# Other start columns for the two halves of the split weights, by group

## The chip, the cores and the metric

The kernel runs on one core of a Trainium2 chip. The metric is device time in microseconds (us), from the start to the end of one execution; lower is better. The time before is the median of three runs, 2103.79 us (2103.69 to 2105.68).

## The reference, cut to what matters

Two layers of a hybrid block, on 256 tokens of width 2048, all in float32. Each layer normalises, projects, mixes in three ways (spatial gating, attention in a window, mLSTM), projects back, and ends in a gated feed-forward part of width 5632:

```python
def hybrid_layer(x, ...):
    hn = rmsnorm(x, norm1_g)
    proj = hn @ w_in                          # 2048 -> 4360
    a_u, a_v, b_q, b_k, b_v, c_qk, c_v, c_o, c_i, c_f = jnp.split(proj, split_idx, axis=-1)
    ...
    mixed = jnp.concatenate([mix_a, mix_b, mix_c], axis=-1)
    h = x + mixed @ w_out                     # 2048 -> 2048
    hn2 = rmsnorm(h, norm2_g)
    return h + (jax.nn.silu(hn2 @ w_gate) * (hn2 @ w_up)) @ w_down   # 2048 -> 2 x 5632 -> 2048
```

Nearly all the arithmetic is in these five products with weights, some 190 MB of weights per layer.

## The kernel before, in words

**Splitting.** TensorE multiplies in a rounded float32 format (fp32r). To keep float32 accuracy each weight and each activation is used as a sum of a high part and a low part. Weights arrive by DMA as `raw` tiles of 128 x 2048 values. `wsplit` (L184 to L193) takes 1024 columns at a time, called a split here: ScalarE (ACT) casts them to the high part `wh` (L191), VectorE (DVE) subtracts that from `raw` to get the low part `wl` (L192).

**The ring.** `wh` and `wl` are two long tiles (L180) of `NSPLIT * SK * CW + LINE` = 4128 columns of 4 bytes. They hold four places for splits, used in turn: split number `i` modulo 4 writes the columns from `i * 1024 + o`, where `o` is an offset that `PLACE` (L41) gives for `wh` and for `wl`, by the form of the product that will read the split:

```python
PLACE = dict(A=(20, 20), B=(12, 12), C=(24, 28))
wh, wl = [t[:, i * SK * CW + o:(i + 1) * SK * CW + o] for t, o in zip(parts, PLACE[form])]
```

An offset of one column is 4 bytes, so (24, 28) starts `wh` 96 bytes and `wl` 112 bytes behind a multiple of 4096 bytes from the tile's start.

**The three forms** (`gemm_steps`, L224 to L307) are three ways to multiply by a split. On TensorE one operand is loaded into the array (the weights of the array, a LDWEIGHTS instruction, PEld in the profile), the other one streams through it (MATMUL).

- Form A (`mm_a`, L239 to L249), tokens on the partitions of the result: the activations are loaded, `wh` and `wl` stream, 512 columns each. Three matmuls (a triple) for each block of 128 inputs and 128 tokens.
- Form B (`mm_f`, L269 to L271), features on the partitions: 128 columns of `wh` or `wl` are loaded, 256 tokens stream. Three matmuls for each block.
- Form C (`mm_f`, L265 and L266): 128 columns of `wh` are loaded and the high and the low activations stream behind one another, 512 columns; then 128 columns of `wl` are loaded and the 256 high activations stream. Two matmuls (a pair) for each block.

**Which group uses which.** A group is one product by 512 columns of weights. In each layer, in this order: `c_q`, `c_k` (form B), a small group of 264 columns (form A), `c_v`, the two halves of `b_q`, `a_v` (form A), `a_u` (form B), `c_o` (form A), four groups of `w_out` (three C, one B), then the feed-forward part in two halves: 12 gate and up groups (form C, each with 256 columns of gate and 256 of up), four groups of `w_down`; 10 gate and up groups, four of `w_down`. The loop over gate and up groups is at L995 to L1024, their product at L999. A group of 16 blocks with form C has 64 pairs and uses 8 splits, so each such group starts at the first place of the ring.

**What sets the order.** TensorE takes the matmuls in the order in which the program is written. The splits are written under a raised priority (L189), so that the scheduler puts the cast and the subtraction among the other work of ACT and DVE ahead of need; the exact position comes out of the scheduler. A cast waits until TensorE has read what stood in its columns.

**Activations.** They lie in `xn_sb` (normalised input), in `big` tiles of 8192 bytes per partition, and, for the last gate and up groups of a half, in `slot` tiles of 4224 bytes per partition.

Of the kernel before, what the change touches and what calls it, by code (L numbers as in the profile page):

```python
# [27 lines left out]
CW = 512  # L28
WK = 4
SK = 2  # L30
# [10 lines left out]
PLACE = dict(A=(20, 20), B=(12, 12), C=(24, 28))  # L41
# [7 lines left out]
OFF = dict(a_u=0, a_v=512, b_q=1024, b_k=2048, b_v=2176, c_q=2304, c_k=2816, c_v=3328, c_o=3840, c_i=4352, c_f=4356)  # L49
G_CQ, G_CK, G_CV, G_Q0, G_Q1, G_AV, G_AU, G_CO = range(8)  # L50
GROUP_COLS = [OFF["c_q"], OFF["c_k"], OFF["c_v"], OFF["b_q"], OFF["b_q"] + 512, OFF["a_v"], OFF["a_u"], OFF["c_o"]]


_p = 0
# [18 lines left out]
def hybrid(ctx: ExitStack, tc: tile.TileContext, xt, win, wsm, wout, wgu, wdn, prm, cst, fgb, yt):  # L73
# [48 lines left out]
    def kchunks(w, order=None):  # L122

        order = range(KT // WK) if order is None else order
        return [(w[c], list(range(c * WK, (c + 1) * WK))) for c in order]
# [54 lines left out]
    parts = [wp.tile([P, NSPLIT * SK * CW + LINE], F32R, tag=k, name=k) for k in ("wh", "wl")]  # L180
    split_no = [0]
    last_split = [None]

    def wsplit(raw, lo, n, form, pieces=1):  # L184
        i = split_no[0] % NSPLIT
        split_no[0] += 1
        wh, wl = [t[:, i * SK * CW + o:(i + 1) * SK * CW + o] for t, o in zip(parts, PLACE[form])]
        m = n // pieces
        with tc.high_priority(HIPRI):  # L189
            for i in range(0, n, m):  # L190
                A.copy(wh[:, i:i + m], raw[:, lo + i:lo + i + m])  # L191
                last_split[0] = V.tensor_tensor(wl[:, i:i + m], raw[:, lo + i:lo + i + m],  # L192
                                                wh[:, i:i + m].bitcast(F32), op=ALU.subtract)  # L193
        return wh, wl
# [9 lines left out]
    def gemm(*args, **kw):  # L204

        steps = gemm_steps(*args, **kw)
        while True:
            try:
                next(steps)
            except StopIteration as end:  # L210
                return end.value
# [9 lines left out]
                    out[i] = end.value  # L221
        return [out[i] for i in range(len(steps))]

    def gemm_steps(form, chunks, xs, cols=CW, ready=None, step0=SK, split=0):  # L224

        ps = [bank(), bank()] if split else gbank()
        if form == "C":
            up = [bank(), bank()]
            tiles = [ps[:, 0:512], ps[:, 512:1024], up[0], up[1]]
        nk = sum(len(k) for _, k in chunks)
        done = 0

        def mm_a(wh, wl, j, kt, first, last, cs=range(NC)):  # L239
            xh, xl = xs(kt)  # L240
            h = wh[:, j * cols:(j + 1) * cols]
            lo = wl[:, j * cols:(j + 1) * cols]
            for c in cs:
                o = ps[c][:, 0:cols] if split else ps[:, c * 512:c * 512 + cols]
                xhc = xh[:, c * P:(c + 1) * P]
                xlc = xl[:, c * P:(c + 1) * P]
                T.matmul(o, xhc, h, start=first, stop=False)  # L247
                T.matmul(o, xhc, lo, start=False, stop=False)  # L248
                T.matmul(o, xlc, h, start=False, stop=last)  # L249

        def mm_first(wh, wl, kt):

            xh, xl = xs(kt)
            for i, (w, x) in enumerate(((wh, xh), (wh, xl), (wl, xh))):
                for f in range(4):
                    T.matmul(ps[:, f * S:(f + 1) * S], w[:, f * P:(f + 1) * P], x, start=i == 0 and f % 2 == 0,
                             stop=False, skip_group_check=True)

        def mm_f(wh, wl, j, kt, f, first, last):
            xh, xl = xs(kt)  # L260
            h = wh[:, j * CW + f * P:j * CW + (f + 1) * P]
            lo = wl[:, j * CW + f * P:j * CW + (f + 1) * P]
            if form == "C":
                o = tiles[f]
                T.matmul(v3(o, 2), h, xs(kt, True), start=first, stop=False, skip_group_check=True)  # L265
                T.matmul(o[:, 0:S], lo, xh, start=False, stop=last, skip_group_check=True)  # L266
            else:
                o = ps[:, f * S:(f + 1) * S]
                T.matmul(o, h, xh, start=first and f % 2 == 0, stop=False, skip_group_check=True)  # L269
                T.matmul(o, h, xl, start=False, stop=False, skip_group_check=True)  # L270
                T.matmul(o, lo, xh, start=False, stop=last, skip_group_check=True)  # L271

        second = []
        for ci, (src, kts) in enumerate(chunks):
            apart = ci >= len(chunks) - split
            raw, step = wload(src, len(kts) * cols), step0 if ci == 0 else SK
            late = form != "A" and ci == len(chunks) - 1
            held = []
            for s0 in range(0, len(kts), step):
                ks = kts[s0:s0 + step]  # L280
                wh, wl = wsplit(raw, s0 * cols, len(ks) * cols, form, 2 if done == 0 and ready is ready_x else 1)
                if ready is not None:
                    ready(ks)
                for j, kt in enumerate(ks):
                    first, last = done == 0, done == nk - 1
                    done += 1
                    if form == "A":
                        mm_a(wh, wl, j, kt, first, last, range(1) if apart else range(NC))
                        if apart:
                            second.append((wh, wl, j, kt, first, last))  # L290
                    elif late:
                        held.append((wh, wl, j, kt, first, last))
                    elif first and ready is ready_x:
                        mm_first(wh, wl, kt)
                    else:
                        for f in range(4):
                            mm_f(wh, wl, j, kt, f, first, last)
                if not late:
                    pump()
                if step0 == 1 and ci == 0 and s0 + step < len(kts):  # L300
                    yield
            if late:
                for f in range(4):
                    for wh, wl, j, kt, first, last in held:
                        mm_f(wh, wl, j, kt, f, first, last)
                    if f % 2 == 1:
                        pump()  # L307
            if ci < len(chunks) - 1:
                yield
        for a in second:  # L310
            mm_a(*a, range(1, NC))
        return (ps, up[0], up[1]) if form == "C" else ps
# [624 lines left out]
    for l in range(DEPTH):  # L937
# [1 line left out]
        st = {}  # L939

        def inproj(i, form):
            return gemm(form, kchunks(win[l, i]), xn)

        if l == 0:
            start(rstd_of(st, True))
            ps, ps1 = in_turn(gemm_steps("B", kchunks(win[l, G_CQ]), xn, ready=ready_x, step0=1),
                              gemm_steps("B", kchunks(win[l, G_CK]), xn, step0=1))
        else:
            start(rstd_of(st))
            ps = inproj(G_CQ, "B")  # L950
# [16 lines left out]
        ps = inproj(G_AU, "B")  # L967
# [23 lines left out]
        for half, (c0, c1) in enumerate(HALVES):  # L991
# [3 lines left out]
            for g in range(ng):  # L995
                if half == 0 and g == 0:
                    st = {}
                    start(rstd_of(st))
                ps, u0, u1 = gemm("C", kchunks(wgu[l, 2 * c0 + g]), xn)  # L999
                need(st, "rbc")  # L1000
                rbc = st["rbc"]
                ts = slot()
                t = ts[:, 0:1024]
                pv = v3(ps, 2)
                A.copy(v3(t[:, 0:512], 2), pv[:, :, S:2 * S])
                V.tensor_tensor(v3(t[:, 0:512], 2), pv[:, :, 0:S], v3(t[:, 0:512], 2), op=ALU.add)
                for j, u in enumerate((u0, u1)):
                    tj = t[:, 512 + j * S:512 + (j + 1) * S]
                    A.copy(tj, u[:, S:2 * S])
                    V.tensor_tensor(tj, u[:, 0:S], tj, op=ALU.add)  # L1010
                V.tensor_tensor(v3(t, 4), v3(t, 4), bc4(rbc), op=ALU.mult)
                A.activation(t[:, 0:512], t[:, 0:512], AF.Silu)
                V.tensor_tensor(t[:, 0:512], t[:, 0:512], t[:, 512:1024], op=ALU.mult)
                if g >= 2 * NBIG:
                    a = slot(F32R)
                    small_act.append(a)
                    av = a[:, 0:1024].rearrange("p (k i t) -> p k i t", k=2, i=2)
                else:
                    if g % 2 == 0:
                        pair = big()  # L1020
                    av = pair[:, 2 * (g % 2):2 * (g % 2) + 2]
                A.copy(av[:, :, 0, :], v3(t[:, 0:512], 2))
                V.tensor_tensor(av[:, :, 1, :], v3(t[:, 0:512], 2), av[:, :, 0, :].bitcast(F32), op=ALU.subtract)
                release(ts)  # L1024
                act.append(av)
# [116 lines left out]
```

## Time and profile before

| what | value |
| --- | --- |
| median of three runs | 2103.79 us (2103.69 to 2105.68) |
| the profiled execution's own time | 2104.66 us |
| its span, first to last instruction | 2102.9 us |
| TensorE busy in the span | 2091.1 us (99%), 12492 matmuls |
| TensorE weight loads busy | 1845.9 us (88%) |
| VectorE / ScalarE busy | 1330.2 us (63%) / 1014.5 us (48%) |
| mean granted TensorE clock | 0.999 of 2.4 GHz |
| DMA | 390.78 MB, mean 186 GB/s |

TensorE's matmuls overlap: one starts while its predecessor still drains, so a matmul that the profile gives 390 ns adds less than that to the time. What a matmul costs is read from the distance between two starts, or from the length of a stretch that holds a known number of them. The table's last rows are shares of a span in which TensorE is nearly always busy; whether the other engines matter is read from what TensorE waits for.

### The profile page before, as it was taken

The numbers are of one execution on the slowest core, as the hardware profiler recorded it, in microseconds if no ns is written. First come the engines' busy times: TensorE is split into PE (matmuls) and PEld (weight loads), VectorE is DVE, ScalarE is ACT, GpSimd is POOL, SyncE is SP. The second block draws the span as 40 slices with busy tenths as digits, with TensorE's granted clock in tenths as the row PEclk, the third lists the DMA queues.
The fourth block names the chain that finished last, engine by engine and source line by source line (L and its number), as shares of the span: only waits on it lengthen the run. The fifth ranks groups of instructions, "written<-read, shape, count | busy, mean of one in ns | idle before, by whom it ended". The sixth has DMA issues, their size and how long they took to land.

```text
span 2102.9 us, 30395 instructions
## 1 busy us (share of the span) xinstructions
PE 2091.1 (99%) x12492; PEld 1845.9 (88%) x12492; DVE 1330.2 (63%) x1827; ACT 1014.5 (48%) x1334; POOL 9.1 (0%) x14
## 2 busy tenths in 40 slices
PE   9999999999999999999999999999999999999998
PEld 9888899888888888888998888988888888888886
DVE  6776666656654566566566766666665555656695
ACT  5655544544443344444445554454444433444443
POOL 0000000000000000000000000000000000000000
PEclk9999999999999999999999999999999999999999
DMA  6544555555555555555546435555555555555653
GB/s 255 211 140 151 177 187 191 187 199 184 198 186 195 182 199 185 196 188 193 184 144 215 141 131 190 191 190 189 191 195 187 199 181 199 186 195 188 212 192 128
DMA packets 56731, 390.78 MB, mean 186 GB/s; under 512 B 6544, under 2 KB 7312, under 8 KB 10512
## 3 DMA queue, kind: packets, MB, share of 16 engines
q1 hardware_dynamic: 56304, 388.33, 52.8%
q8 instruction: 97, 1.59, 0.3%
q10 hardware_dynamic: 288, 0.52, 0.1%
q14 instruction: 42, 0.34, 0.0%
HBM read 386.73 MB, written 2.10 MB: 185 GB/s over the span
## 4 chain that ended last, share of the span: by engine, by line
PE 99%; DVE 0%; issue 0%; DMA 0%; ACT 0%; SPq 0%; POOLq 0%; DVEq 0%; POOL 0%
PE g L265 22%; PE m L265 22%; PE g L266 11%; PE m L266 11%; PE g L247 5%; PE g L248 5%; PE g L249 5%; PE g L269 4%; PE g L271 4%; PE g L270 4%; PE m L566 1%; PE m L620 1%; PE m L609 1%; PE m L247 0%; PE m L248 0%; PE m L249 0%
## 5 line engine op out<-in xcount | busy, mean ns | idle before, releaser
L192 DVE TENSOR_TENSOR wl<-raw,wh 128x1024 fp32r<-128x1024 f32 (+2 forms) x741 | 886.7, 1205 | 600.6 <-ACT wh L191 592.2
L191 ACT CAST wh<-raw 128x1024 fp32r<-128x1024 f32 (+2 forms) x741 | 758.8, 1033 | 865.5 <-PE m L265 528.8
L265 PE MATMUL g<-xn_sb,wh 128*128 128x512 f32 x1408 | 510.8, 390 | 0.0
L265 PE MATMUL m<-xn_sb,wh 128*128 128x512 f32 x1408 | 510.8, 390 | 0.0
L266 PE MATMUL g<-xn_sb,wl 128*128 128x256 f32 x1408 | 391.8, 278 | 0.0
L266 PE MATMUL m<-xn_sb,wl 128*128 128x256 f32 x1408 | 391.8, 278 | 0.0
L265 PEld LDWEIGHTS m<-xn_sb,wh 128*128 128x128 f32 x1408 | 264.3, 188 | 55.5
L265 PEld LDWEIGHTS g<-xn_sb,wh 128*128 128x128 f32 x1408 | 264.2, 188 | 55.4
L266 PEld LDWEIGHTS m<-xn_sb,wl 128*128 128x128 f32 x1408 | 264.3, 188 | 0.1
L266 PEld LDWEIGHTS g<-xn_sb,wl 128*128 128x128 f32 x1408 | 264.3, 188 | 0.1
L265 PE MATMUL g<-big,wh 128*128 128x512 f32 x512 | 187.7, 391 | 0.0
L265 PE MATMUL m<-big,wh 128*128 128x512 f32 x512 | 187.4, 390 | 0.0
L247 PE MATMUL g<-wh,xn_sb 128*128 128x512 f32 (+1 forms) x384 | 147.8, 385 | 0.0
L248 PE MATMUL g<-wl,xn_sb 128*128 128x512 f32 (+1 forms) x384 | 143.8, 375 | 0.0
L249 PE MATMUL g<-wh,xn_sb 128*128 128x512 f32 (+1 forms) x384 | 143.4, 373 | 0.0
L266 PE MATMUL g<-big,wl 128*128 128x256 f32 x512 | 142.7, 279 | 0.0
L266 PE MATMUL m<-big,wl 128*128 128x256 f32 x512 | 142.7, 279 | 0.0
L265 PEld LDWEIGHTS m<-big,wh 128*128 128x128 f32 x512 | 96.1, 188 | 20.4
L265 PEld LDWEIGHTS g<-big,wh 128*128 128x128 f32 x512 | 96.1, 188 | 20.4
L269 PE MATMUL g<-xn_sb,wh 128*128 128x256 f32 x380 | 109.7, 289 | 0.0
L271 PE MATMUL g<-xn_sb,wl 128*128 128x256 f32 x380 | 107.4, 283 | 2.2 <-DVE wl L192 2.2
L270 PE MATMUL g<-xn_sb,wh 128*128 128x256 f32 x380 | 106.8, 281 | 0.0
(246 smaller groups left out, 2555.0 us busy)
## 6 DMA issues: line engine op xcount, KB each, us to landing
raw<-in_wgu SPq DMA_DIRECT2D x176, 1024.0 KB, 4.8
raw<-in_wdn SPq DMA_DIRECT2D x88, 1024.0 KB, 4.8
raw<-in_win SPq DMA_DIRECT2D x62, 1024.0 KB, 4.8
raw<-in_wout SPq DMA_DIRECT2D x32, 1024.0 KB, 4.7
raw<-in_wsm SPq DMA_DIRECT2D x8, 528.0 KB, 3.4
raw<-in_win SPq DMA_DIRECT2D x7, 256.0 KB, 6.5
out_yt<-end SPq DMA_DIRECT2D x4, 384.0 KB, 3.0
hT<-in_xt SPq DMA_DIRECT2D x1, 1024.0 KB, 10.5
```

What stands on the lines that cost most here:

```text
L191: A.copy(wh[:, i:i + m], raw[:, lo + i:lo + i + m])
L192: last_split[0] = V.tensor_tensor(wl[:, i:i + m], raw[:, lo + i:lo + i + m], wh[:, i:i + m].bitcast(F32), op=ALU.subtract)
L247: T.matmul(o, xhc, h, start=first, stop=False)
L248: T.matmul(o, xhc, lo, start=False, stop=False)
L249: T.matmul(o, xlc, h, start=False, stop=last)
L265: T.matmul(v3(o, 2), h, xs(kt, True), start=first, stop=False, skip_group_check=True)
L266: T.matmul(o[:, 0:S], lo, xh, start=False, stop=last, skip_group_check=True)
L269: T.matmul(o, h, xh, start=first and f % 2 == 0, stop=False, skip_group_check=True)
L270: T.matmul(o, h, xl, start=False, stop=False, skip_group_check=True)
L271: T.matmul(o, lo, xh, start=False, stop=last, skip_group_check=True)
L566: T.matmul(o, x[r, sl], k[g][r, 0:n], start=i == 0, stop=i == 2, skip_group_check=True)
L609: T.transpose(b[:, p * P:(p + 1) * P], pslice(c, 2 * p + par)[:, blk * P:(blk + 1) * P], ident)
```

## The change

The offsets are no longer given by the form alone. `wsplit` takes the pair of offsets as an argument. The 22 gate and up groups get eleven different pairs, one for each two groups, the same in both layers. Of the groups of form A the five of 512 columns in the input projection get five pairs in layer 0 and five others in layer 1; one of the ten, `c_v` of layer 0, is (20, 20) as before. All other groups keep `PLACE`.

```diff
+GU_PLACE = ((26, 30), (24, 26), (24, 30), (24, 32), (28, 28), (28, 32), (26, 28), (22, 28), (20, 28), (28, 24), (24, 20))
+A_PLACE = ({G_CV: (20, 20), G_Q0: (18, 18), G_Q1: (22, 22), G_AV: (4, 4), G_CO: (8, 8)},
+           {G_CV: (19, 19), G_Q0: (21, 21), G_Q1: (20, 24), G_AV: (24, 20), G_CO: (32, 32)})
...
-    def wsplit(raw, lo, n, form, pieces=1):
+    def wsplit(raw, lo, n, place, pieces=1):
         i = split_no[0] % NSPLIT
         split_no[0] += 1
-        wh, wl = [t[:, i * SK * CW + o:(i + 1) * SK * CW + o] for t, o in zip(parts, PLACE[form])]
+        wh, wl = [t[:, i * SK * CW + o:(i + 1) * SK * CW + o] for t, o in zip(parts, place)]
...
-    def gemm_steps(form, chunks, xs, cols=CW, ready=None, step0=SK, split=0):
+    def gemm_steps(form, chunks, xs, cols=CW, ready=None, step0=SK, split=0, place=None):
...
-                wh, wl = wsplit(raw, s0 * cols, len(ks) * cols, form, 2 if done == 0 and ready is ready_x else 1)
+                wh, wl = wsplit(raw, s0 * cols, len(ks) * cols, place or PLACE[form], 2 if done == 0 and ready is ready_x else 1)
...
-            return gemm(form, kchunks(win[l, i]), xn)
+            return gemm(form, kchunks(win[l, i]), xn, place=A_PLACE[l].get(i))
...
-                ps, u0, u1 = gemm("C", kchunks(wgu[l, 2 * c0 + g]), xn)
+                ps, u0, u1 = gemm("C", kchunks(wgu[l, 2 * c0 + g]), xn, place=GU_PLACE[c0 + g // 2])
```

No instruction is added or removed. TensorE's matmuls stand in the same order. In the mixing stages of both layers the scheduler puts some casts and subtractions a few instructions earlier or later on ACT and DVE; in the gate and up groups their order is unchanged.

The place with the largest such move is on ACT, in the attention of layer 0. `raw_157` holds the first weights of `a_u`; the rows at L580 (L585 in the change) are exponentials of the attention's scores. Before:

```order
97 L580 ACTIVATE slot_149_1586,den_148_1585<-slot_149_1586,nmx_146_1583 128x128
98 L191 CAST wh_73<-raw_157_1671 128x1024
99 L577 ACTIVATE es_147_1584<-es_147_1584 128x8
100 L580 ACTIVATE slot_149_1586,den_148_1585<-slot_149_1586,nmx_146_1583 128x128 x7
101 L191 CAST wh_73<-raw_157_1671 128x1024
```

And in the change, where every line number is higher by 5:

```order
98 L585 ACTIVATE slot_149_1586,den_148_1585<-slot_149_1586,nmx_146_1583 128x128
99 L582 ACTIVATE es_147_1584<-es_147_1584 128x8
100 L585 ACTIVATE slot_149_1586,den_148_1585<-slot_149_1586,nmx_146_1583 128x128 x7
101 L196 CAST wh_73<-raw_157_1671 128x1024
102 L582 ACTIVATE es_147_1584<-es_147_1584 128x4
```

The first cast of `raw_157` has moved behind eight short activations.

## Rows read from the trace of the kernel before

**Rows 1.** The page: busy time of TensorE, and the chain that ended last.

```profile
PE 2091.1 (99%) x12492; PEld 1845.9 (88%) x12492; DVE 1330.2 (63%) x1827; ACT 1014.5 (48%) x1334; POOL 9.1 (0%) x14
...
PE 99%; DVE 0%; issue 0%; DMA 0%; ACT 0%; SPq 0%; POOLq 0%; DVEq 0%; POOL 0%
```

**Rows 2.** Waits of TensorE, first 25 us (none later): us in total, times, longest.

```profile
PE g L271 <- DVE wl L192: 2.2, 4, 1.5
PE m L336 <- DVE ones L333: 1.1, 1, 1.1
```

**Rows 3.** The page's costliest groups: count, busy us, mean ns, idle before them.

```profile
L192 DVE TENSOR_TENSOR wl<-raw,wh 128x1024 fp32r<-128x1024 f32 (+2 forms) x741 | 886.7, 1205 | 600.6 <-ACT wh L191 592.2
L191 ACT CAST wh<-raw 128x1024 fp32r<-128x1024 f32 (+2 forms) x741 | 758.8, 1033 | 865.5 <-PE m L265 528.8
L265 PE MATMUL g<-xn_sb,wh 128*128 128x512 f32 x1408 | 510.8, 390 | 0.0
L266 PE MATMUL g<-xn_sb,wl 128*128 128x256 f32 x1408 | 391.8, 278 | 0.0
```

**Rows 4.** Timeline of TensorE inside a gate and up group: start us, us, instruction.

```profile
400.14 0.39 PE L265 MATMUL m<-xn_sb,wh 128*128 128x512 f32 x1
400.36 0.28 PE L266 MATMUL m<-xn_sb,wl 128*128 128x256 f32 x1
400.48 0.39 PE L265 MATMUL m<-xn_sb,wh 128*128 128x512 f32 x1
400.71 0.28 PE L266 MATMUL m<-xn_sb,wl 128*128 128x256 f32 x1
400.82 0.39 PE L265 MATMUL g<-xn_sb,wh 128*128 128x512 f32 x1
```

**Rows 5.** Stretches of form C: start:end, length us, TensorE busy, clock, DMA.

```profile
367.86:389.84 21.98, 21.98 (x131) 1.00 0.55 194
1961.61:1983.58 21.97, 21.97 (x131) 1.00 0.56 193
587.60:609.57 21.97, 21.97 (x131) 1.00 0.54 191
609.57:620.75 11.18, 11.18 (x66) 1.00 0.56 196
620.75:643.22 22.47, 22.47 (x130) 1.00 0.53 187
```

**Rows 6.** Stretches of form B, two groups of w_down in layer 0.

```profile
995.88:1024.59 28.71, 28.71 (x242) 1.00 0.53 188
1024.59:1052.89 28.30, 28.30 (x243) 1.00 0.52 184
```

**Rows 7.** Stretches of form A, w_down of layer 1, activations in big, then slot.

```profile
1983.58:2005.66 22.08, 22.08 (x98) 1.00 0.59 207
2005.66:2011.26 5.60, 5.60 (x25) 1.00 0.68 212
```

**Rows 8.** Groups of TensorE by line and shape in the mLSTM, 108 to 122 us.

```profile
L790 PE MATMUL m<-slot,slot 128*128 128x128 f32 x8 | 1.1, 275 | 0.0
L814 PE MATMUL m<-slot,slot 128*128 128x129 f32 x8 | 1.1, 274 | 0.0
```

**Rows 9.** Timeline of ACT in the attention of layer 0.

```profile
168.23 1.03 ACT L191 CAST wh<-raw 128x1024 fp32r<-128x1024 f32 x1
169.17 0.21 ACT L577 ACTIVATE es<-es 128x8 f32<-128x8 f32 x1
...
171.60 0.39 ACT L580 ACTIVATE slot<-slot,nmx 128x128 f32<-128x128 f32 x1
171.89 0.19 ACT L580 ACTIVATION_READ_ACCUMULATOR slot<-slot,nmx 128x1 f32 x1
```

**Rows 10.** Timeline of TensorE at the first matmul of the group a_u.

```profile
180.47 0.28 PE L269 MATMUL g<-xn_sb,wh 128*128 128x256 f32 x1
```

## The prediction

> **What bounds the kernel now.** I read the page first: TensorE is busy for 2091.1 of 2102.9 us and the chain that ended last is TensorE for 99% of the span [rows 1]. Then I read the waits of TensorE: 2.2 us for a low part that was not written yet and 1.1 us at the very start, all in the first 25 us, and none after [rows 2]. So no other engine and no transfer sets the end, and the time is the sum of the distances between starts of matmuls. The change leaves all matmuls, their order and their sizes. It can move the time in two ways only: it makes TensorE wait for a split, or it changes how long a matmul takes because its operands lie at other addresses.
>
> The reader should see next what a matmul costs, and that this depends on addresses. In a gate and up group the starts are 0.22 to 0.23 us apart behind a 512-column matmul and 0.11 to 0.12 us behind a 256-column one [rows 4], less than the durations of 390 and 278 ns [rows 3], which overlap. A whole group is 64 pairs in 21.97 us, or 343.3 ns a pair. The third and the last group cost the same to 0.01 us [rows 5], and so do those in between, but for the first of each layer, which has other matmuls among its own. So this cost is not jitter: the same addresses give the same time.
>
> Other addresses give another one. The first group of `w_down` in layer 0 is form C with the same offsets. While its activations come from `big`, 64 pairs take 21.97 us, 343.3 ns each. When they come from `slot` tiles, 32 pairs take 11.18 us, 349.4 ns each [rows 5]. And the next group, the same instructions from `big` at the same addresses, takes 22.47 us for its first 64 pairs, 351.1 ns each [rows 5]. So the pairs can run in more than one rhythm, a rhythm keeps itself up for a whole stretch, and which one is taken depends on addresses and on how the stretch was entered. Form B shows two rhythms as well: 80 blocks in 28.71 and in 28.30 us, 358.9 and 353.8 ns a block [rows 6]. Form A: 32 triples in 22.08 us from `big`, 690.0 ns, but 8 triples in 5.60 us with activations in `slot`, 700 ns [rows 7]. The clock is 1.00 in all of these, so it is not the clock.
>
> What the rhythm is made of no row tells. My reading is that the load for the next matmul and the stream of the running one read the same memory at the same time, and that their relative address decides how often one holds up the other.
>
> **The change part by part.** *Waits for splits.* Where the offset grows from one group to the next, a new split reaches into the first columns of the next place of the ring, read three splits earlier instead of four. A cast may start one split later than before. A split of a gate and up group lasts TensorE 8 pairs x 343.3 ns = 2.75 us. Cast and subtraction take 1.03 + 1.21 = 2.24 us [rows 3]; after the wait two splits, 5.5 us, are still ahead of need. So I take 0; without that cover it would be up to 2.24 us at each place where an offset grows (a rival below). Where the offset shrinks, the columns were freed earlier.
>
> *Moved casts.* The first cast of `a_u`'s weights ran from 168.23 to 169.26 us and now stands behind activations that ended at 172.08 [rows 9], so it ends about 3 us later. Its first reader is the first matmul of `a_u`, at 180.47 us [rows 10], 11.2 us after the old end. 0 again; its subtraction, 1.21 us, still fits. The splits behind it on ACT are later by at most as much, and they are read later still. The other moves in the mixing stages shift a cast by fewer instructions than this one; I take them as 0.
>
> *Gate and up groups.* An entry of the table serves two groups in two layers, 4 x 64 = 256 pairs, so 1 ns a pair is 0.256 us an entry and 2.82 us over all eleven. No row shows a pair at a new offset, so I bound it by the rows that differ in address or rhythm. Dear end: all eleven at 351.1 ns, 7.8 ns more, 22.0 us. Cheap end: the gain between form B's two rhythms, 5.1 ns a block of three matmuls, scaled to two matmuls: 3.4 ns a pair, 9.6 us less over all. Between them: the present rhythm is the cheapest of the three form C stretches in [rows 5], so leaving it costs more often than it gives. Of the eleven entries three change both offsets by which the two loads of a pair meet their stream, (26, 30), (28, 32) and (28, 24); the other eight keep one of 24 and 28. I choose: those three leave the rhythm, and two of the eight. A leaving entry costs the mean of the two seen, 6.1 and 7.8 ns: 6.95 x 256 = 1.78 us. Five of them: **+8.9 us**.
>
> Some of the offsets are no multiple of four columns, so these parts start inside a 16-byte line. The nearest row on that is the mLSTM: its 129-wide operands lie 516 bytes apart, three of four off a 16-byte boundary, and take 274 ns beside 275 ns for aligned 128-wide ones [rows 8]. I put no extra on it. The Trainium skill's page SBUF — State Buffer (Specifications) speaks of 16-byte cachelines, where each step to a new line pays a penalty; by it a load of 512 bytes that starts inside a line touches 33 lines and not 32, at worst 1/32 more of a load, and the (26, x), (22, 28) and (24, 26 or 30) entries would all be somewhat slower. The row above does not bear that out for streams; no row shows it for loads.
>
> *Form A groups.* Nine of ten change, 9 x 32 = 288 triples. Dear end: 10 ns each as in [rows 7], 2.9 us. Cheap end: a triple is three matmuls as a form B block is, so 5.1 ns less, 1.5 us. I take half the dear end, 5 ns: **+1.4 us**.
>
> *Groups not touched.* A group behind a changed one may be entered in the other rhythm, as the two `w_down` groups show: 22.47 - 21.97 = 0.5 us each, either sign. I take 0.
>
> Sum: 8.9 + 1.4 = 10.3 us. Against the profiled execution's 2104.66 us (2102.9 span, 1.8 around it) that is 2115.0; it stands 0.9 us above the median of the runs, so against the median 2103.79 it is 2114.1. **I forecast 2114.0 us**, 0.5% slower. About 0.2% (4.2 us) is what a measurement of this kernel can tell from no change.
>
> **The rivals.** *No change, about 2104.* The change would not do anything if the two reads never met. For it: within a form the gate and up groups, with 22 sets of weights, agree to 0.01 us. Against it: the stretches from `slot` and the second rhythm at 1.00 clock [rows 5, 7]. It also covers the case that eight or more entries keep the rhythm: two that leave cost 3.6 us, still within the bound. The skill's page SBUF — State Buffer (Who interferes with whom) would have it so: TensorE's port for the stream and its port for loads are independent. 25%.
>
> *Faster, about 2097.* The mechanism is the same, but the present pair of offsets is not a good one: a rhythm below 343.3 ns exists near it. It decides if more entries gain than lose. With a gain of 3.4 ns x 256 = 0.87 us an entry, net seven winning entries give 6.1 us and 2097.7. For it: inside form B the same addresses have a rhythm that is 1.4% cheaper. Against it: no form C stretch is under 343.3 ns. 14%.
>
> *Slower by waits.* Offsets grow at 19 group borders where they did not before (7 in each layer from the gate and up groups on, 5 among the form A groups). If the overlap made the cast wait for the split just before it, TensorE would stand up to 2.24 us at each: 19 x 2.24 = 43 us at most, 2146. It decides if fewer than 2.24 us of cover are left; I count 5.5. For it: four waits for `wl` exist already, but all lie in the first 25 us, where the ring is being filled [rows 2]. 3%.
>
> **How the numbers follow.** Forecast 58%, waits 3%, no change 25%, faster 14%. Slower by over 0.2%: 0.61; within: 0.25; faster: 0.14. The range reaches down through the no-change case and the edge of the faster one, 2099, which leaves out some 12%; upward the dear ends give 2103.8 + 22.0 + 2.9 = 2128.7, which needs all entries to leave, so I stop at 2125 and leave out 8%.
>
> **What would show it.** In the profile after, waits of TensorE stay at about 3 us and the clock at 1.00. Gate and up groups take steps in length by entry: most at 21.97 us, about five entries at 22.3 to 22.5 us, the same in both layers. Form A groups lengthen by some 0.2 us. If all groups keep 21.97 us the no-change rival holds. Groups under 21.9 us speak for the faster one; TensorE waiting for `wh` or `wl` at group borders for the last one. I am wrong if the lengths differ between the layers at the same offsets, or if untouched groups carry the difference.

## The result and the profile after

| what | before | after |
| --- | --- | --- |
| median of the runs | 2103.76 us (4 runs, 2103.69 to 2105.68) | 2126.35 us (4 runs, 2125.36 to 2126.84) |
| the profiled execution's own time | 2104.66 us | 2126.01 us |
| its span | 2102.9 us | 2124.2 us |
| TensorE busy | 2091.1 us | 2112.5 us |
| mean granted TensorE clock | 0.999 | 0.999 |

The changed kernel takes 1.0104 times as long, interval 1.0092 to 1.0116. The forecast was 2114.0, the range ended at 2125: the direction was right, the forecast of 10 us was less than half of the 22.6 us that came.

The page of the kernel after, its busy times, its chain and the two costliest groups of TensorE, beside [rows 1, 3] (every line number is higher by 5):

```profile
PE 2112.5 (99%) x12492; PEld 1853.6 (87%) x12492; DVE 1330.7 (63%) x1827; ACT 1014.7 (48%) x1334; POOL 9.1 (0%) x14
...
PE 98%; DVE 0%; issue 0%; DMA 0%; SPq 0%; ACT 0%; DVEq 0%; POOLq 0%; POOL 0%; ACTq 0%
...
L270 PE MATMUL g<-xn_sb,wh 128*128 128x512 f32 x1408 | 518.5, 395 | 0.0
...
L271 PE MATMUL g<-xn_sb,wl 128*128 128x256 f32 x1408 | 395.3, 281 | 0.0
```

TensorE is still nearly the whole chain (98%, before 99%), with as many matmuls as before. They are longer: 395 ns where 390 stood, and 281 where 278 stood. DVE and ACT are busy as long as before.

The waits of TensorE in the kernel after (us in total, times, longest), beside [rows 2]:

```profile
PE g L276 <- DVE wl L197: 1.9, 3, 1.5
PE m L341 <- DVE ones L338: 1.1, 1, 1.1
PE g L274 <- ACT wh L196: 0.2, 1, 0.2
```

These are the waits at the start of the program; no border between two offsets has brought one. So all of the time went into the distances between matmuls.

Stretches of the kernel after (start:end, length, TensorE busy, clock, DMA). The first seven are one group each of gate and up, to be read beside 21.97 us [rows 5]; the last two are groups of `w_down` that the change did not touch:

```profile
346.69:369.09 22.40, 22.40 (x130) 1.00 0.52 185
413.47:435.94 22.47, 22.47 (x131) 1.00 0.54 190
525.40:548.01 22.61, 22.61 (x130) 1.00 0.54 184
838.81:861.56 22.75, 22.75 (x130) 1.00 0.53 175
1892.84:1915.59 22.75, 22.75 (x130) 1.00 0.53 179
928.69:950.88 22.19, 22.19 (x131) 1.00 0.54 190
950.88:978.91 28.03, 28.03 (x163) 1.00 0.54 188
1681.06:1714.74 33.68, 33.68 (x194) 1.00 0.54 186
```

These are the entries (26, 30), (24, 30) and (28, 28), then (20, 28) in both layers and (24, 20). The layers agree to 0.01 us, the clock is 1.00, and **not one entry kept 21.97**. From the starts of their matmuls the entries took, in the order of the table: 22.40, 22.19, 22.47, 22.19, 22.61, 22.62, 22.44, 22.18, 22.76, 22.47 and 22.19 us.

Summed over all groups, each from its first matmul to the next group's first: the 44 gate and up groups are 18.9 us longer, the ten groups of form A 1.45 us, the two untouched `w_down` groups 0.54 us (27.49 before) and 0.63 us (33.05 before). These make 21.5 us. The span grew by 21.3; the rest are pieces of 0.3 us and less of both signs, the largest in the first 55 us.

ACT and DVE write `wh` and `wl` and transfers fill `raw` while TensorE reads, and the writes of `wh` and `wl` move with the offsets too. They are not what keeps the pairs long. A pair of the entry (28, 28) during which DVE, ACT and POOL do nothing and no transfer runs (here with all engines: PE, PEld, DVE, ACT, POOL, clock, DMA):

```profile
522.22:522.57 0.35, 0.35 (x4) 0.31 (x3) 0.00 (x0) 0.00 (x0) 0.00 (x0) 1.00 0.00 0
```

Four pairs of this group have ACT and DVE idle throughout; they take 353, 353, 354 and 354 ns, and the mean of the group is 353.2. In (24, 30) it is four pairs at 351 ns beside a mean of 351.1. So the longer pace stands without any writing to `wh`, `wl` or `raw` beside it.

### The profile page after: what moved, and what is told of

It reads as the page before. It is cut to its first block, busy times and chain, and to the rows that moved or that the text cites. A ratio compares the mean times of both kernels' runs of the same rounds, so it can differ in the third digit from the quotient of the medians.

```text
span 2124.2 us, 30387 instructions
## 1 busy us (share of the span) xinstructions
PE 2112.5 (99%) x12492; PEld 1853.6 (87%) x12492; DVE 1330.7 (63%) x1827; ACT 1014.7 (48%) x1334; POOL 9.1 (0%) x14
## 4 chain that ended last, share of the span: by engine, by line
PE 98%; DVE 0%; issue 0%; DMA 0%; SPq 0%; ACT 0%; DVEq 0%; POOLq 0%; POOL 0%; ACTq 0%
PE g L270 22%; PE m L270 22%; PE g L271 11%; PE m L271 11%; PE g L252 5%; PE g L253 5%; PE g L254 5%; PE g L274 4%; PE g L276 4%; PE g L275 4%; PE m L571 1%; PE m L625 1%; PE m L614 1%; PE m L252 0%; PE m L253 0%; PE m L254 0%
## 5 line engine op out<-in xcount | busy, mean ns | idle before, releaser
L270 PE MATMUL g<-xn_sb,wh 128*128 128x512 f32 x1408 | 518.5, 395 | 0.0
L270 PE MATMUL m<-xn_sb,wh 128*128 128x512 f32 x1408 | 518.5, 395 | 0.0
```

## The experiments

A time without an interval is that of one execution; beside these the kernel before took 2103.9 to 2105.0 us on the same chips. The lengths of the groups, which repeat to some hundredths of a microsecond, tell more than the totals. A pair of offsets names a group's entry; an offset of 4 columns is 16 bytes. Where a diff says "as the change", the offsets come by argument from a table.

**All three moved together.** The weights' parts and the activations in `xn_sb` 16 bytes earlier, so that their distances are those of the change.

```diff
-    xn_sb = cp.tile([P, KT, 2, S], F32R, tag="xn", name="xn_sb")
+    xn_all = cp.tile([P, 512 + KT * 2 * S], F32R, tag="xn", name="xn_sb")
+    xn_sb = xn_all[:, 508:508 + KT * 2 * S].rearrange("p (k i t) -> p k i t", k=KT, i=2)
+GU_PLACE = ((22, 26), (20, 22), (20, 26), (20, 28), (24, 24), (24, 28), (22, 24), (18, 24), (16, 24), (24, 20), (20, 16))
```

> The normalised activations lie 16 bytes (4 columns) earlier, and every offset of the gate and up table is 4 columns less; the tiles behind the activations lie 2048 bytes later. Theory, the distance between the loaded part and the streamed activations decides: each entry keeps the length it had in the change, by entry 22.40, 22.19, 22.47, 22.19, 22.61, 22.62, 22.44, 22.18, 22.76, 22.47, 22.19 us a group, within 0.03. Rival, the parts' own addresses decide: entries take the length of the offsets they now have, so the sixth, now (24, 28), falls to 21.97 and the fourth, now (20, 28), rises to 22.76.

It took 2125.98 us. Groups of its fourth, fifth and sixth entries:

```profile
480.18:502.79 22.61, 22.61 (x130) 1.00 0.52 179
502.79:525.54 22.75, 22.75 (x130) 1.00 0.55 192
548.30:570.49 22.19, 22.19 (x130) 1.00 0.55 189
```

By the distances these would be 22.19, 22.61 and 22.62 us; by the parts' own places the sixth, (24, 28), would be 21.97. Both theories miss. Neither the place of the parts alone decides, nor, for a move of 16 bytes, the distance alone.

**Only the activations moved.** The kernel before with the first three lines of that diff.

> The kernel before with all offsets as they were, but the normalised activations 16 bytes earlier (tiles behind them 2048 bytes later). Theory, the distance decides: the distance is that of (28, 32) in the change, so all gate and up groups behind the first of a layer take 22.62 us in place of 21.97, some 28 us in all. Rival, the parts' own addresses decide: 21.97 us as before.

2116.14 us. A gate and up group:

```profile
413.89:436.08 22.19, 22.19 (x130) 1.00 0.53 190
```

Neither of the lengths that the theories named. But the parts, what ACT and DVE write, and all offsets are those of the kernel before, and the groups are still 0.22 us dearer. So it is not the parts' address for the engines that write them: the address of TensorE's other operand counts too. The pad also puts the tiles behind the activations 2048 bytes later, which is eight times the 256 bytes at which the map below finds the lengths repeated.

**The order of the entries.** One entry for all of layer 0, the table backwards in layer 1.

```diff
-                ps, u0, u1 = gemm("C", kchunks(wgu[l, 2 * c0 + g]), xn, place=GU_PLACE[c0 + g // 2])
+                ps, u0, u1 = gemm("C", kchunks(wgu[l, 2 * c0 + g]), xn, place=(20, 28) if l == 0 else GU_PLACE[10 - c0 - g // 2])
```

> Layer 0: all 22 gate and up groups at (20, 28), so no offset changes between them. Layer 1: the change's table in reversed order. Theory: in layer 0 every group behind the first takes 22.76 us, in layer 1 the lengths go with the entry, 22.19, 22.47, 22.76, 22.18, 22.44, 22.62, 22.61, 22.19, 22.47, 22.19, 22.40 us. Rival, the borders between unlike offsets or the neighbours cost the time: layer 0 at 21.97 us, and layer 1 unlike the change's lengths.

2126.18 us. A group of layer 0, then from layer 1 (20, 28) and (24, 30):

```profile
414.57:436.87 22.30, 22.30 (x131) 1.00 0.54 190
1467.52:1489.81 22.29, 22.29 (x130) 1.00 0.54 191
1869.47:1891.94 22.47, 22.47 (x130) 1.00 0.53 187
```

With no border at all, all groups of layer 0 are 0.32 us dearer than 21.97. So borders are not what costs. In layer 1 eight of the eleven entries kept the length that they have in the change; (20, 28) went from 22.76 to 22.30, (24, 32) from 22.19 to 22.40, (26, 30) from 22.40 to 22.61. The same addresses have more than one rhythm. What ran before or the place in the program chooses; the last run below has both rhythms at the same places of the two layers.

**A map.** Layer 0 holds `wh` at 24 and moves `wl`, layer 1 holds `wl` at 28 and moves `wh`, in steps of 4 columns, and then by 64, 128 and 256 columns.

```diff
-    parts = [wp.tile([P, NSPLIT * SK * CW + LINE], F32R, tag=k, name=k) for k in ("wh", "wl")]
+    parts = [wp.tile([P, NSPLIT * SK * CW + 288], F32R, tag=k, name=k) for k in ("wh", "wl")]
+DN_PLACE = ((32, 32), (19, 19), (52, 52), (20, 52))
...
-                    ps = gemm("A", down_chunks(l, q, half), act_x, split=2 if q == 3 else 0)
+                    ps = gemm("A", down_chunks(l, q, half), act_x, split=2 if q == 3 else 0, place=DN_PLACE[q])
```

> A map: one offset pair for each of the 44 gate and up groups. Layer 0: wh at 24 and wl at 0, 4, ... 60, then wl at 92 and 156, then both moved by 32, 64 and 128. Layer 1: wl at 28 and wh at 0, 4, ... 60, 88, 152, then both, one and the other moved by 256. Form A input groups at (32, 32) in layer 0 and (19, 19) in layer 1; the last four down groups at (32, 32), (19, 19), (52, 52), (20, 52). Theory: the length is a function of the distance that repeats; by the slot stretches (128 bytes apart, 349.4 ns a pair) a move of both by 32 columns gives 22.36 us and moves by 64 or more columns give 21.97 again; the known points come back, (24, 20) and (24, 32) 22.19, (20, 28) 22.76, (28, 28) 22.61. At least one point below 21.97 would show that the offsets of before are not the best. Rival, groups differ by what stands before them: the known points do not come back.

2123.35 us. Groups at (24, 24), (24, 28), (24, 156), then in layer 1 (24, 28) and (280, 284):

```profile
479.16:501.56 22.40, 22.40 (x131) 1.00 0.54 187
501.56:523.53 21.97, 21.97 (x130) 1.00 0.53 192
858.00:879.97 21.97, 21.97 (x130) 1.00 0.54 185
1528.51:1550.99 22.48, 22.48 (x130) 1.00 0.54 189
1929.38:1951.36 21.98, 21.98 (x131) 1.00 0.62 221
```

One step of 16 bytes in one part takes the group from 21.97 to 22.40 us. Moved by 64, 128 or 256 columns, one part alone or both, it is back at 21.97 to 21.99: for this pair the lengths repeat at 256 bytes. Both parts moved by 32 columns, (56, 60), took 22.47 us where 22.36 was expected. Of the four known points three came back; (20, 28) took 22.29 us, its other length. In layer 1, behind (20, 28), the old pair itself took 22.48 us.

This run also shows the wait that the change was spared. The last four groups of layer 1 (form A, 10 splits each, so that the second and the fourth start at the third place of the ring) took 28.60 to 30.74 us in place of 27.45 to 27.68, the last one counted to the start of its last matmul. The waits of TensorE have new rows, 4.1 us in all:

```profile
PE g L254 <- DVE wl L198: 1.3, 1, 1.3
PE m L253 <- ACT wh L197: 1.1, 1, 1.1
PE g L253 <- ACT wh L197: 1.1, 1, 1.1
PE m L254 <- DVE wl L198: 0.6, 1, 0.6
```

They stand at two borders, at 2024 and 2084 us, where the offset shrinks, from (32, 32) to (19, 19) and from (52, 52) to (20, 52). The first split of the new group then begins inside the last columns of the split just before it, and its cast waits until TensorE has read that one. ACT and TensorE at the first of the two borders:

```profile
2023.10 1.99 ACT L197 CAST wh<-raw 128x1024 fp32r<-128x1024 f32 x2 [1.76 <-PE g L255]
2024.19 0.50 PE L253 MATMUL g<-wh,big 128*128 128x512 f32 x1 [1.13 <-ACT wh L197]
```

At the border between them, at 2055 us from (19, 19) to (52, 52), the offset grows and the group starts at the first place: no wait. The first and the third group have no wait and still took 28.89 and 29.22 us; that part, 2.7 us, is rhythm.

**The frame moved by 256 and 128 bytes, then by 64 and 32.** The activations of the feed-forward part start later; the parts are at pairs that keep or break the distance, and form A has its offsets of before.

```diff
+    xn_all = cp.tile([P, 256 + KT * 2 * S], F32R, tag="xn", name="xn_sb")
+        return xn_all[:, o:o + KT * 2 * S].rearrange("p (k i t) -> p k i t", k=KT, i=2)
...
+        x_at[0] = [64, 32][l]
```

> All form A and B groups at the offsets of before. The normalised activations of the feed-forward part start 64 columns (256 bytes) later in layer 0 and 32 columns (128 bytes) later in layer 1. Since the joint move by 16 bytes did not keep the lengths, the theory is now: the length is set by where the stream and each of the two loads lie in a frame of 256 bytes, by all three and not by their distances alone. It expects in layer 0 the lengths of unmoved activations: 21.97 us at (24, 28), 22.19 at (24, 32), 22.61 at (28, 28), 22.62 at (28, 32), 22.44 at (26, 28), 22.19 at (22, 28), 22.29 or 22.76 at (20, 28); in layer 1 no return to 21.97 us at (56, 60), where all three have moved by 128 bytes. Rival, a frame of 128 bytes or less: (56, 60) takes 21.97 us. Second rival, the pad itself changed the lengths in the earlier runs: layer 0 does not come back to 21.97 us.

2119.32 us. With the activations 256 bytes later, (24, 28) is at 21.97 us, as without the move, but at 22.48 when it comes behind (24, 32); of the other lengths expected there one failed, (28, 32) at 22.33 us and not 22.62:

```profile
390.39:412.36 21.97, 21.97 (x131) 1.00 0.52 186
568.45:590.93 22.48, 22.48 (x131) 1.00 0.54 187
```

With the activations 128 bytes later (layer 1), (56, 60), which keeps the distance, took 22.46 to 22.48 us in all its groups behind the first, the other length of (24, 28), and not 21.97.

The second run has `x_at[0] = [16, 8][l]`.

> The activations of the feed-forward part 16 columns (64 bytes) later in layer 0 and 8 columns (32 bytes) later in layer 1, with a sweep of offsets round (40, 44) and (32, 36), the offsets of before moved along. Theory (frame of 256 bytes, all three places count): the joint moves do not return to 21.97 us, and the offset of the activations alone, at (24, 28), leaves it as well. Rival, a frame of 64 or 32 bytes: (40, 44) or (32, 36) takes 21.97 us. A group under 21.95 us anywhere would show that 21.97 us is no floor.

2122.78 us. With the activations 32 bytes later (layer 1), first (24, 28) left where it was, then (32, 36), which keeps the distance; then, with the activations 64 bytes later (layer 0), (40, 44), which keeps the distance, and (40, 28), the dearest group of all:

```profile
1400.74:1423.36 22.62, 22.62 (x131) 1.00 0.48 169
1445.34:1467.32 21.98, 21.98 (x131) 1.00 0.56 193
391.80:414.28 22.48, 22.48 (x130) 1.00 0.54 188
436.89:459.89 23.00, 23.00 (x130) 1.00 0.51 187
```

Of 19 distances measured at 32 bytes, 17 have a length of the same distance in the map to 0.02 us; of 18 at 64 bytes, 13; of 8 at 128 bytes, 7. Two different distances agree as closely in 26%, 16% and 5% of the cases, so this is more than chance. Of the 11 that were moved by 16 bytes in the first run, none has its length of the change. So what decides, as far as these runs go, is the distance between what is loaded and what streams, under moves by 32 bytes and its multiples, and beside it the rhythm in which the group was entered. The other eight may differ by that, for several distances have two lengths in these runs, but that is not shown; I found no rule that foretells which.

**Two more maps.** 44 more groups each at other pairs, odd columns among them; forms A and B get other offsets too. Only the tables differ, with `A_PLACE` extended to form B, and the arguments that hand them on.

> Activations where they were. 44 more offset pairs for the gate and up groups: equal offsets, 4, 16 and 32 apart, and odd ones next to (24, 28). Theory: all lie above 21.97 us, at 22.1 to 22.8, since no column next to (24, 28) kept the rhythm in the change; odd columns are no dearer than even ones. Rival: (24, 28) is one of several good pairs, and some groups take 21.97 us or less. Form A: the last four down groups at (19, 19), no waits there, some 27.4 us each in place of 27.68, by the 0.11 to 0.18 us a group that (19, 19) gave in the input projection; other form A and B offsets are tried once each, with no number expected.

2118.67 us. Groups at (48, 32), (24, 40) and (25, 29):

```profile
1976.67:1998.44 21.77, 21.77 (x131) 1.00 0.56 199
1820.09:1842.07 21.98, 21.98 (x131) 1.00 0.55 190
769.65:791.86 22.21, 22.21 (x131) 1.00 0.55 190
```

(48, 32) is below the 21.97 of the kernel before, the first pair that is. Odd columns lie among the others: (25, 29) 22.20, (23, 27) 22.33, (24, 29) 22.61. Form A's last groups took 27.47 us at (19, 19), and form B's groups of `w_down` 28.24 us at (28, 28).

> A third map of 44 offset pairs, round (48, 32), which gave 21.77 us once, and at the same distance of 16 columns elsewhere, with (48, 32) itself five times behind different neighbours. Theory: (48, 32) gives 21.77 us each time or one other fixed length, if it has a second rhythm; (24, 40), 21.98 us once and 22.54 in a shifted frame, shows two lengths. Rival: 21.77 was owed to the place in the program, and (48, 32) gives 21.97 or more elsewhere. Form A and B: (51, 51) in the last four down groups below 27.68 us, form B at (28, 32) in two down groups near 28.24 us.

2114.95 us. (48, 32) right behind the first group of layer 0, the same pair later (five groups of it took 21.77 or 21.78 us), and (48, 36):

```profile
344.97:367.37 22.40, 22.40 (x130) 1.00 0.52 181
501.28:523.05 21.77, 21.77 (x130) 1.00 0.55 190
746.37:768.14 21.77, 21.77 (x131) 1.00 0.54 190
```

Over the change and the three maps, 106 different pairs (modulo 64 columns) were measured. Their mean is 22.35 us. Four were ever seen at 21.99 us or below: (24, 28), (24, 40), (48, 32) and (48, 36). Form A's last groups took 27.47 to 27.51 us at (51, 51); form B at (28, 32) took 28.29 and 28.48 us, above the 28.24 that was expected.

**The size of the slot tiles.** If distances repeat at 256 bytes, tiles of 4224 bytes (16.5 times 256) put every second `slot` at another distance.

```diff
-SLOT = 1056
+SLOT = 1088
```

> The kernel before with slot tiles of 4352 bytes (17 x 256) in place of 4224 (16.5 x 256), offsets as before. If distances repeat at 256 bytes, the stretches with activations in slot get the pace of those in big, 343.3 ns a pair: the four groups of w_down in the first half take 32.96 us each (96 pairs) in both layers, where before they took 33.16 and 33.62 us in layer 0 and 33.05 us in layer 1; the gate and up groups stay at 21.97; the time falls by about 2 us, to 2102. If slot is slower for another reason than its distance, these groups keep their lengths and the time stays at 2104.

2103.09 us beside 2103.99. A group of `w_down` in layer 0, one in layer 1, then the first of the two of form B:

```profile
587.70:620.66 32.96, 32.96 (x194) 1.00 0.54 192
1630.77:1663.72 32.95, 32.95 (x194) 1.00 0.55 191
994.21:1023.01 28.80, 28.80 (x243) 1.00 0.54 187
```

The length of form C came out as worked out, 96 x 343.3 ns, in all eight groups. The total fell by 0.9 us and not by 2: form B entered a dearer rhythm, 28.80 us twice in place of 28.71 and 28.30 [rows 6], which the expectation had not reckoned with.

**Form A's part of the change alone.** As the change, without the table for gate and up.

> The change without its gate and up table: form C is back at (24, 28) everywhere, only the nine new offsets of form A stay. Theory (each group's length comes from its own offsets): gate and up groups back at 21.97 us, form A groups as in the change, together 1.4 us more than before, so about 2105.2 us, and the two down groups that had lengthened behind the table (28.03 and 33.68 us) back at 27.49 and 33.05. Rival, the mere switching between offsets costs: a good part of the 22 us stays.

2105.58 us beside 2104.13, ratio 1.0008 (0.9998 to 1.0017), which is no difference that the times alone can show. A gate and up group, and the untouched `w_down` group that had taken 28.03:

```profile
543.40:565.38 21.98, 21.98 (x131) 1.00 0.56 191
940.64:968.13 27.49, 27.49 (x162) 1.00 0.55 192
```

Everything outside the form A groups is back to 0.1 us, but for the first 55 us and the first `w_out` group of layer 1, and the form A groups have the lengths of the change: the 18.9 us and the 1.2 us on untouched groups belong to the gate and up table.

**A better version.** The kernel before, without any table, at the cheapest pair of the maps.

```diff
-SLOT = 1056
+SLOT = 1088
-PLACE = dict(A=(20, 20), B=(12, 12), C=(24, 28))
+PLACE = dict(A=(19, 19), B=(28, 32), C=(48, 32))
-    parts = [wp.tile([P, NSPLIT * SK * CW + LINE], F32R, tag=k, name=k) for k in ("wh", "wl")]
+    parts = [wp.tile([P, NSPLIT * SK * CW + 96], F32R, tag=k, name=k) for k in ("wh", "wl")]
```

> The kernel before with one offset pair for each form, chosen from the maps: A (19, 19), B (28, 32), C (48, 32), and slot tiles of 4352 in place of 4224 bytes, so that all of them lie alike in a frame of 256 bytes. Theory, per group as in the maps: 44 gate and up groups 0.20 us less each, 6 groups of w_out 0.20, the down groups of form C 0.3 to 0.9 with the slot stretches at the pace of big, form B groups 0.3 to 0.5, form A groups 0.1 to 0.2; in all some 20 us less, about 2083 us, ratio 0.990. Rival, single groups of a map do not carry over to a whole program because the rhythm depends on how a group is entered: a ratio between 0.996 and 1.010.

2083.24 us (2083.08 to 2083.76) beside 2104.13, **ratio 0.99, interval 0.9884 to 0.9917**. A gate and up group, a `w_down` group of form C, one of form B and one of form A:

```profile
386.25:408.00 21.75, 21.75 (x130) 1.00 0.53 192
582.08:614.72 32.64, 32.64 (x194) 1.00 0.55 193
984.64:1012.92 28.28, 28.28 (x242) 1.00 0.54 190
1990.55:2018.01 27.46, 27.46 (x121) 1.00 0.60 210
```

64 pairs in 21.76 us are 340.0 ns a pair, and the 96 pairs of the second line have the same pace, with the activations in `slot` too. Of the 21.3 us between the two traces 9.3 lie in the gate and up groups, 6.5 in the other groups of form C, 2.3 in form B, 2.2 in form A and 1.0 in the first 55 us.

**The better version with the old slot tiles.** As above with `SLOT = 1056`.

> The better version with the slot tiles left at 4224 bytes. If the distance decides, the gate and up groups stay at 21.76 us and only the groups of w_down with activations in slot, and form A's, lose their pace: 32.64 us becomes some 33.0 to 33.7, about 4 us in all, 2087. If the slot tiles have no part in it, 2083.

2095.34 us, 8 more than expected. A gate and up group of layer 0 and one of layer 1, both at (48, 32):

```profile
456.54:478.94 22.40, 22.40 (x130) 1.00 0.54 187
1495.66:1517.42 21.76, 21.76 (x130) 1.00 0.57 194
```

All eleven groups behind the first in layer 0 took 22.40 us, those of layer 1 and of layer 0's second half 21.76 or 21.77, in one execution and at the same addresses. Form A kept its pace (27.47). The expected loss was too small because it left out the entrance: eleven groups times 0.64 us are 7.0 us. The groups of form C in `w_down` lost 2.9 us beside the better version, where some 4 were expected of them and form A together, and the first 56 us took 1.8 us more. So a rhythm, once entered, stays for as long as like groups follow, and the addresses of the group itself do not settle which one it is.

## Why the prediction missed

- *TensorE sets the end, no waits, moved casts at 0.* Held: the waits are 3.2 us in all, before 3.3, and ACT and DVE stayed off the chain. One reason given was wrong, though: "Where the offset shrinks, the columns were freed earlier." That holds here only because every group whose offset shrinks starts at the first place of the ring. At the third place the map shows the wait, 4.1 us at two borders, and none where the offset grew, which is where the rival had put it.
- *The price of an entry that leaves the rhythm*, 6.95 ns a pair, 1.78 us an entry. Held as a mean: 18.9 us over 44 x 64 = 2816 pairs is 6.7 ns a pair, 1.72 us an entry. Single entries went from 3.4 ns, (24, 26), to 12.3 ns, (20, 28); the dear end of 7.8 ns was no bound for one entry, but the mean stayed under it. That the mean of two other stretches came so near to the mean of eleven new pairs is in part luck.
- ***The count: this step failed.*** "I choose: those three leave the rhythm, and two of the eight." All eleven left. Eleven times 1.78 us would have been 19.6, and 2125 in all. The choice rested on the thought that a pair which keeps 24 or 28 keeps half of what matters. The map refutes it: one part moved by 16 bytes is enough, in either direction. I had the evidence for a higher count in hand, for I wrote that the present rhythm was the cheapest of the form C stretches, and still gave six of eleven entries the lucky case. Among 106 pairs it was reached by four.
- *Form A groups*, +1.4 us, half of the dear end. Measured +1.45: the size was right, though single groups went from -0.12 to +0.46 us.
- *Groups not touched*, taken as 0 with 0.5 us each as the bound. Two came out, both upwards, +0.54 right behind a group of the table and +0.63 one group later: 1.2 us.
- *No extra for starts inside a 16-byte line.* Held: in the change the five entries with such a start took 22.18 to 22.47 us, the six without 22.19 to 22.76; in the maps (25, 29) took 22.20 us and (24, 24) 22.40. The Trainium skill's page SBUF — State Buffer (Specifications (TRN2)) has each cross to a new 16-byte line pay a penalty. These lengths do not show one for such starts.
- *The rivals.* "No change" rested on the reads not meeting, and all eleven entries refute it: 21.76 to 23.00 us over all runs, at one clock and with one set of instructions. The Trainium skill's page SBUF — State Buffer (Who interferes with whom) calls the two read ports of TensorE, for the stream and for loads, independent. Read as the prediction reads it, every pair would take the same time, and the traces differ from that; whether it is the ports that meet or something behind them no row shows. "Faster" did not come, but its premise was true: a cheaper rhythm lay at (48, 32), 24 and 4 columns away, and no row of before pointed to that pair. "Waits" did not come; the map's last four groups show that they exist, at shrinking offsets inside the ring.

The upper end of the range was cut for the same reason as the forecast: 2128.7 "needs all entries to leave", which I held to be rare and which came.

What stays open: which reads or cells meet inside the memory was not seen. Writes by ACT and DVE and transfers are ruled out as what keeps the pace up, by the pairs that run without them. That the load and the stream disturb each other is the reading that fits the repeat at 256 bytes, the joint moves and the activations moved alone; it is argued, for no row shows a single conflict. And no run foretells which rhythm an entrance chooses.

## What to carry to other kernels

Where TensorE is busy all the time and its matmuls are back to back, the start of each operand modulo 256 bytes can be a tuning parameter, worth about 1% in either direction here (ratios 1.0104 and 0.99): fix the distances, keep every tile that feeds the same product at a multiple of 256 bytes, sweep the pairs in one run by giving each group another one, and read the lengths of the groups, not the total. When a tuned placement is disturbed in many places at once, count every place as lost, unless a row shows that one is not. Where buffers overlap in a ring, look at the border where a start moves back onto the buffer just used. Judge a candidate by the groups before and behind it as well, for the rhythm in which a stretch is entered can cost as much as the placement gives.

## What the runs showed that I had not expected

- The same 64 pairs of instructions take 21.76 to 23.00 us (340.0 to 359.4 ns a pair) at a clock of 1.00, by addresses and by what ran before, and in the change they repeat to 0.02 us between layers.
- One placement can hold two rhythms, 21.76 and 22.40 us, for eleven groups in a row each, in one execution.
- 128 bytes in the size of a tile that these groups do not read (the slot tiles) changed which rhythm eleven of them were in, by what ran ahead of them: 7.0 of the 12 us between 2095.34 and 2083.24 us.
